# Rounding tiles to 256 bytes, staggering the compression between dense products, and taking one group of value products last

## The chip, the cores and the metric

The kernel runs on one core of a Trainium2 chip. It computes a hybrid attention layer and two further transformer layers for 512 tokens of width 1024, in float32. The metric is the device time of one execution in microseconds; the time before is the median of three runs.

## The reference, cut to what matters

```python
def hybrid_layer(x, mem, ...):
    x = x + 0.5 * swiglu_ffn(rmsnorm(x, ffn1_norm_g), ffn1_w_in, ffn1_w_out)     # d_ff = 2816
    h = rmsnorm(x, mix_norm_g)
    q, kv, nsa_g, conv_in, q_mem, merge_g = jnp.split(h @ w_in, split_points, axis=-1)
    kc, vc, ks, vs, kw, vw = ...                      # 4 groups of 64 columns each, 16 query heads
    k_cmp = rmsnorm(compress(kc, cmp_pe_k, cmp_w1_k, cmp_w2_k), k_norm_g)  # 31 blocks of 32 tokens, stride 16
    v_cmp = compress(vc, cmp_pe_v, cmp_w1_v, cmp_w2_v)      # silu(flat @ w1) @ w2
    o_nsa = nsa_attention(...)    # gated sum of compressed, selected and window attention
    o_conv = short_gated_conv(conv_in, conv_w, conv_b)
    o_mem = memory_attention(q_mem, mem, ...)               # 256 memory slots, 4 heads
    x = x + (g_nsa * o_nsa + g_conv * o_conv + g_mem * o_mem) @ w_out
    return x + 0.5 * swiglu_ffn(rmsnorm(x, ffn2_norm_g), ffn2_w_in, ffn2_w_out)

def second_block(x, p, ...):
    # layer 0: stick-breaking attention, layer 1: forgetting attention (softmax of q k + f_q - f_k);
    # both followed by swiglu and by h + sigmoid(rms_norm(h) @ w_gate) * (p @ w_proj)
```

## The kernel before

Everything lies transposed: 1024 features are eight tiles of 128 partitions, 512 tokens are the columns. A product in float32 precision is made of three matmuls: each operand is split into a rounded high part and the rest (`split`: ScalarE writes the high part, VectorE the difference), and `mm3` takes high by high, high by low and low by high. `dense` and `job` are the dense products: 128 rows of weights arrive by one DMA of 512 KB on SP's queue into a `raw` tile, are split into `wh` and `wl` (`weights`, three buffers each), and 24 matmuls of 512 columns follow, in which the stationary operand is a slice of `wh` or `wl` and the moving operand one of the sixteen tiles `h0h`, `h0l` ... `h7l` (the normalized activations). The second products of a feed-forward move the tiles `u0h` ... `u21l` (66 matmuls), `project` the tiles `m0h` ... `m7l`.

The stages follow one another: memory keys, feed-forward 1 (`ffn`), `memory`, `nsa`, `merge`, feed-forward 2, `stick`, feed-forward 3 with `ple`, `forget`, feed-forward 4 with `ple`. In `nsa` and `forget` dense products are cut into steps of three matmuls (`job`, `job_tok`) that `feed(n)` and `pace(upto)` put between the attention's instructions; `begin` starts their list, and each job's weights are asked for when the job before it starts. An attention loop runs over units (one head and one branch): `unit_scores`, softmax, `unit_scale` on GpSimd, and one unit later `unit_turn` (transposes and split of the probabilities) and `unit_out` (value products). In the loop the order of TensorE's instructions is that of the code (`pinned`); ahead of it the scheduler of the language may take what is ready first. `compress` is a generator: each `next(comp)` issues one more part of the compression of the keys and then the values. `nsa_cmp` does the same for the compressed scores of one group, in three parts.

A tile is given its place by its pool: tiles lie one behind another along the partition in the order of their first use, each as long as its width rounded up (`t`). `sb` is the first pool and holds `cols` (226 columns), `ones_d` (128), `eps` (one column) and then the sixteen `h` tiles; `wp`, with `raw`, `wh` and `wl`, follows behind `sb`. Pools on the right lie below a tile `edge` of 24 columns. In the program built of this kernel `h0h` begins at byte 2816 of the partition, `wh` at 69504, `u0h` of feed-forward 1 at 139136, `m0h` at 112512 in `merge`. The pools of `stick` and `forget` begin with the tile `rT` of four columns. In `memory` the tiles `mt` and `vm` lie an odd multiple of 256 bytes apart, by that program.

Of the kernel before, what the change touches and what calls it, by code (L numbers as in the profile page):

```python
# [28 lines left out]
LV = 1040  # L29
LU = 384  # L30


# [130 lines left out]
class Net:  # L163
    def __init__(self, ctx, tc, a, out):
        self.tc, self.nc, self.a, self.out = tc, tc.nc, a, out
        self.uid = self.turn = 0
        self.due, self.rest = [], []
        self.jobs, self.steps, self.pinned = None, 0, False
        self.tags = self.TAGS = ("d", "s", "t", "o")

        self.edge = ctx.enter_context(tc.tile_pool(name="edge", bufs=1, side="right"))
        self.edge.tile([P, 24], F32, name="edge", tag="edge")
        self.sb = ctx.enter_context(tc.tile_pool(name="sb", bufs=1))
        self.wp = ctx.enter_context(tc.tile_pool(name="wp", bufs=3))
        self.ps = ctx.enter_context(tc.tile_pool(name="ps", bufs=2, space=bass.MemoryType.PSUM))
        self.dr = ctx.enter_context(tc.tile_pool(name="dr", bufs=1, space=bass.MemoryType.DRAM))

    def t(self, pool, cols, tag, bufs=None, dt=F32, parts=P):
        self.uid += 1
        w = cols if pool is self.ps else -(-cols // 64) * 64 if dt == BF16 else -(-cols // 32) * 32  # L180
        x = pool.tile([parts, w], dt, name=f"{tag}_{self.uid}", tag=tag, bufs=bufs)
        return x if w == cols else x[:, :cols]
# [438 lines left out]

    def softmax_rows(self, pool, src, n, bias, stat, tag, bufs):

        nc = self.nc
        m = self.t(pool, 1, "sm", 8)
        p = self.t(pool, n, tag, bufs)
        if bias is None:
            nc.vector.tensor_reduce(m, src, axis=AX, op=ALU.min)
            nc.scalar.activation(p, src, AF.Exp, bias=m, scale=-1.0, accum_out=stat)
        else:  # L630
            nc.vector.tensor_tensor_reduce(  # L631
                out=p, in0=src, in1=bias, op0=ALU.add, op1=ALU.min, scale=1.0, scalar=3e38, accum_out=m)
            nc.scalar.activation(p, p, AF.Exp, bias=m, scale=-1.0, accum_out=stat)  # L633
        return p
# [47 lines left out]
    def memory(self):  # L682

        nc, tc = self.nc, self.tc
        with self.pool("mem", "left") as pool:
# [10 lines left out]
            for m in range(4):  # L696
# [15 lines left out]
                self.split(vm[0], vm[1], vr)  # L712
                st = self.t(pool, NT, "mst", 2)
                pr = []
                for i in range(NT):
                    sc = self.bank("s")[:, :NM]
                    q = slice(i * P, (i + 1) * P)
                    for c in range(2):
                        self.mm3(sc, qr[c][0][:, q], qr[c][1][:, q], kr[c][0], kr[c][1], c == 0, c == 1)
                    pr.append(self.softmax_rows(pool, sc, NM, None, st[:, i : i + 1], "mp", 8))  # L720
                nc.vector.reciprocal(st, st)
                pt = []
# [77 lines left out]
    def compress_flat(self, pool, tn, xs):  # L800
# [3 lines left out]
        ph = self.bank("o")[:, :256]  # L804
        for k in range(4):
            fl = self.t(pool, S, "cv", 4)
            fv = fl.rearrange("p (k g c) -> p k g c", g=4, c=32)
            nc.vector.memset(fl.rearrange("p (k c) -> p k c", c=32)[:, :, 31:], 0.0)
            for g in range(4):
                xa = xs[g // 2][64 * (g % 2) : 64 * (g % 2) + 64, :]  # L810
                for par in range(2):
                    h = slice(64 * par, 64 * par + 64)
                    xv = bass.AP(xa.tensor, xa.offset + par + 8 * k, [list(xa.ap[0]), [2, 4], [16, 31]])
                    nc.vector.tensor_tensor(  # L814
                        fv[h, :, g, :31], xv, pe[h, 4 * k : 4 * k + 4].unsqueeze(2).to_broadcast([64, 4, 31]), op=ALU.add)
# [62 lines left out]
    def unit_scores(self, pool, b, q, k, bias, mask=None):  # L878

        st = self.t(pool, NT, "st", 4)  # L880
        pr = []
        both = self.bank("s")
        for tiles in ((0, 1), (2,), (3,)):
# [9 lines left out]
            for i in tiles:  # L893
                n = (i + 1) * P
                pr.append(self.softmax_rows(pool, sc[i][:, :n], n, bias(n), st[:, i : i + 1], f"pr{i}", 2))
        return pr, st

# [17 lines left out]
    def unit_out(self, po, v, pt, first, last):  # L915

        ph, pl = pt
        for j in range(NT):
            n = S - j * P
            c = slice(self.PT0[j], self.PT0[j] + n)  # L920
            self.mm(po[:, j * P :], v(j), pl[:, c], start=first and j == 0, stop=False)
            self.mm(po[:, j * P :], v(j), ph[:, c], start=False, stop=last and j == NT - 1)

    def nsa(self):
        nc, tc = self.nc, self.tc
        self.hv = 1
        with self.pool("nsa", "right") as pool:
# [34 lines left out]
            def key(j):  # L962
                def post(ps):
                    k = self.t(pool, S, f"kx{j}") if j % 2 else self.t(pool, S, "cv", 4)
                    nc.vector.tensor_tensor(k, ps, self.rB, op=ALU.mult)
# [36 lines left out]
            self.feed(6)  # L1002
            for j in range(4):
                self.head_norm(ks[j], j, 1, st, self.col("kg"))
                self.feed(2)
            kn = [keys(0, br) for br in range(2)]
            self.feed(10)
            next(comp)
            st = self.head_stats(raw[0], self.sel64, 1, tag="o", fill=2)
            next(comp)  # L1010
            self.feed(6)
            for r in range(4):
                normed(0, r, st)
                if r == 2:
                    next(comp)
                self.feed(3)
            for _ in comp:
                self.feed(3)
# [12 lines left out]
            self.pace(8 * 12 + 8)  # L1031
            self.pinned = True
# [3 lines left out]
            for u in range(33):  # L1036
# [56 lines left out]

    def nsa_cmp(self, pool, a, b, qn, kc, G, pc):

# [3 lines left out]
        for z, y, w in ((kc[b], self.kcn[0], slice(0, P)), (kc[2 + b], self.kcn[1], h)):  # L1099
# [3 lines left out]
            nc.vector.tensor_copy(dst, y[w, 32 * g : 32 * g + 32].bitcast(F32).unsqueeze(1).to_broadcast([n, 4, 32]))  # L1103
        cb = self.t(pool, S, "cp", 1)
        for r in range(4):
# [9 lines left out]
        for i in range(NT):  # L1115
            self.tr(tp[:, i * P : (i + 1) * P], cb[:, i * P : (i + 1) * P])
        m = self.t(pool, 16, "cm", 2)
        rows = tp.rearrange("p (k c) -> p k c", c=32)
# [3 lines left out]
        nc.scalar.activation(cb, cb, AF.Exp, scale=-1.0)  # L1122
        z = self.t(pool, 16, "cz", 2)
        nc.vector.tensor_reduce(z, pv, axis=AX, op=ALU.add)
# [166 lines left out]
    def forget(self):  # L1291
# [3 lines left out]
        with self.pool("fox", "left") as pool:  # L1295
# [69 lines left out]
            self.feed(6)  # L1365
            base = self.steps
            rows = None
            fb = self.forget_bias(pool, 0)
            for u in range(17):
# [89 lines left out]
```

## Time and profile before

| | us |
|---|---|
| median of three runs | 2975.08 (2967.96 to 2980.09) |
| the profiled execution, its own time | 2973.13 |
| its span, first to last instruction | 2971.2 |
| TensorE (PE) busy in the span | 2898.9 |
| VectorE (DVE) busy | 1628.5 |
| ScalarE (ACT) busy | 1216.9 |
| GpSimd (POOL) busy | 247.9 |

The profiled execution lies 2 us below the median and the span 2 us below its own time. Lines of the profile name an engine, the source line (a helper's: L189 is every matmul, L194 every transpose, L208 and L218 the two halves of `split`), the operation, and output and inputs by tile name without buffer numbers. PEclk or "granted clock" is the share of TensorE's full 2.4 GHz. A matmul's own duration reaches past the start of the next; its pace is the distance from start to start.

### The profile page before, as it was taken

Reading aid. Unit: us, or ns where it says so; the run is one execution under the profiler, and the core shown is the slowest. Engines: PE = TensorE matmul, PEld = TensorE weight load, DVE = VectorE, ACT = ScalarE, POOL = GpSimd, SP = SyncE. Lnnn points to the kernel's source line nnn. Section 1 sums busy time; section 2 is a strip of 40 time slices with the busy share of each in tenths; the row PEclk is TensorE's granted clock in tenths of the full one; section 3 lists DMA queues with packets and bytes.
Section 4 is the critical chain, followed back from the end, with each engine's and each line's share of the span. In section 5 each row is a group of like instructions: output and inputs, shape, how many; then the busy total and the mean of one; then the engine's idle time right before and its main releaser. Section 6 shows DMA issues by size and latency. Waiting matters only on the chain.

```text
span 2971.2 us, 37172 instructions
## 1 busy us (share of the span) xinstructions
PE 2898.9 (98%) x13873; PEld 2369.6 (80%) x13874; DVE 1628.5 (55%) x2718; ACT 1216.9 (41%) x2078; POOL 247.9 (8%) x361
## 2 busy tenths in 40 slices
PE   8999999988999999999999999999999999999999
PEld 7888887766878888888888887888887777888887
DVE  7443345587677665344347877343357767544344
ACT  6322234344555544232235655222234556422223
POOL 0000000001224320000000000000003331000000
PEclk9999999999999999999999999999999999999999
DMA  7423342234333345222344345222334535522332
GB/s 239 107 92 96 104 130 89 96 105 124 94 105 93 91 151 172 97 93 91 112 122 117 86 123 185 97 92 91 97 110 127 141 93 157 180 92 93 94 93 98
DMA packets 133229, 339.19 MB, mean 114 GB/s; under 512 B 17415, under 2 KB 30215, under 8 KB 133048
## 3 DMA queue, kind: packets, MB, share of 16 engines
q1 hardware_dynamic: 132376, 335.49, 37.0%
q10 hardware_dynamic: 672, 1.32, 0.4%
q8 instruction: 109, 1.79, 0.2%
q14 instruction: 72, 0.59, 0.1%
HBM read 279.82 MB, written 28.61 MB: 104 GB/s over the span
## 4 chain that ended last, share of the span: by engine, by line
PE 72%; DVE 5%; issue 3%; ACT 1%; DMA 1%; POOL 0%; SPq 0%; DVEq 0%; POOLq 0%; ACTq 0%
PE d L189 27%; PE s L189 14%; PE o L189 14%; PE t L189 12%; PE t L194 2%; DVE wl L218 1%; DVE cv L814 1%; DMA qk<-xd 0%; DVE ptl L218 0%; DMA xd<-qk 0%; PE s L1278 0%; PE o L1288 0%; PE t L1278 0%; PE o L1289 0%; ACT wh L208 0%
## 5 line engine op out<-in xcount | busy, mean ns | idle before, releaser
L208 ACT ACTIVATE wh<-raw 128x1024 fp32r<-128x1024 f32 (+3 forms) x499 | 493.7, 990 | 1223.3 <-PE d L189 327.1
L218 DVE TENSOR_TENSOR wl<-raw,wh 128x1024 fp32r<-128x1024 f32 (+3 forms) x499 | 573.6, 1150 | 302.7 <-ACT wh L208 291.9
L900 POOL TENSOR_SCALAR pr<-pr,st 128x128 f32<-128x128 f32 x192 | 116.6, 627 | 245.0 <-DVE st L1374 97.8
L633 ACT ACTIVATE pr<-pr,sm 128x128 f32<-128x128 f32 x192 | 106.0, 553 | 64.1 <-DVE sm L631 63.6
L218 DVE TENSOR_TENSOR ptl<-t,pth 128x512 fp32r<-128x512 f32 x144 | 85.6, 596 | 32.6 <-ACT pth L208 30.7
L230 POOL TENSOR_TENSOR raw<-raw,cols 128x1024 f32<-128x1024 f32 x25 | 50.0, 2001 | 538.5 <-DMA xd<-x 472.1
L208 ACT ACTIVATE pth<-t 128x512 fp32r<-128x512 f32 x144 | 75.0, 522 | 48.5 <-PE t L194 47.8
L194 PE MATMUL t<-idn,pr 128*128 128x128 f32 x480 | 78.0, 278 | 3.0 <-DVE ptl L218 2.3
L194 PEld LDWEIGHTS t<-idn,pr 128*128 128x128 f32 x480 | 60.6, 143 | 21.6 <-DVE ptl L218 4.6
L631 DVE CUSTOM_DVE_ANT_0 pr<-s,tb 128x128 f32<-128x128 f32 (+3 forms) x128 | 57.9, 486 | 33.2 <-PE s L189 11.5
L189 PE MATMUL o<-ptl,V 128*128 128x512 f32 x192 | 60.3, 325 | 5.9 <-DVE ptl L218 5.7
L407 POOL MEMSET hrh<- 128x512 f32 (+2 forms) x10 | 4.7, 472 | 661.4 <-DVE wl L218 480.9
L189 PE MATMUL d<-h0h,wh 128*128 128x512 f32 x136 | 56.8, 418 | 0.0
L517 ACT ACTIVATE ta<-ta 128x512 f32<-128x512 f32 x88 | 55.5, 633 | 3.2 <-DVE ta L516 3.0
L189 PE MATMUL d<-h4h,wh 128*128 128x512 f32 x136 | 56.2, 413 | 0.0
L518 DVE TENSOR_TENSOR ta<-s,ta 128x512 f32<-128x512 f32 x22 | 15.2, 692 | 74.6 <-PE s L189 74.6
L189 PE MATMUL d<-h3h,wh 128*128 128x512 f32 x136 | 56.1, 412 | 0.0
L518 DVE TENSOR_TENSOR ta<-t,ta 128x512 f32<-128x512 f32 x22 | 15.2, 692 | 74.1 <-PE t L189 74.0
L189 PE MATMUL o<-pth,V 128*128 128x512 f32 x192 | 55.8, 324 | 0.0
L189 PE MATMUL d<-h2h,wh 128*128 128x512 f32 x136 | 55.5, 408 | 0.0
L482 ACT ACTIVATE on<-o 64x512 f32<-64x512 f32 x48 | 28.6, 595 | 65.8 <-PE o L189 51.1
L189 PE MATMUL d<-h1h,wh 128*128 128x512 f32 x136 | 55.4, 407 | 0.0
(2163 smaller groups left out, 8719.8 us busy)
## 6 DMA issues: line engine op xcount, KB each, us to landing
raw<-in_f_in_dram SPq DMA_DIRECT2D x176, 512.0 KB
raw<-in_f_out_dram SPq DMA_DIRECT2D x64, 512.0 KB
raw<-in_f_out_dram SPq DMA_DIRECT2D x32, 384.0 KB
raw<-in_w_mg_dram SPq DMA_DIRECT2D x24, 512.0 KB
raw<-in_w_cv_dram SPq DMA_DIRECT2D x24, 512.0 KB
xd<-x SPq DMA_DIRECT2D x32, 256.0 KB
x<-xd SPq DMA_DIRECT2D x32, 256.0 KB
raw<-in_w_pg_dram SPq DMA_DIRECT2D x16, 512.0 KB
```

The lines of the kernel that those rows point to most:

```text
L189: i = self.nc.tensor.matmul(out, lhs, rhs, **kw)
L194: i = self.nc.tensor.transpose(out, src, self.ident)
L208: nc.scalar.activation(h, src, AF.Copy, scale=1.0 if scale is None else scale)
L218: eng.tensor_tensor(lo, src, hb, op=ALU.subtract)
L230: nc.gpsimd.tensor_tensor(v, v, gain.unsqueeze(2).to_broadcast([P, gain.shape[1], n]), op=ALU.mult)
L482: self.nc.scalar.activation(dst[h], po[64:], AF.Copy)
L517: nc.scalar.activation(ta, ta, AF.Silu)
L518: nc.vector.tensor_tensor(ta, pb, ta, op=ALU.mult)
L631: nc.vector.tensor_tensor_reduce(out=p, in0=src, in1=bias, op0=ALU.add, op1=ALU.min, scale=1.0, scalar=3e38, accum_out=m)
L633: nc.scalar.activation(p, p, AF.Exp, bias=m, scale=-1.0, accum_out=stat)
L814: nc.vector.tensor_tensor(fv[h, :, g, :31], xv, pe[h, 4 * k : 4 * k + 4].unsqueeze(2).to_broadcast([64, 4, 31]), op=ALU.add)
L900: self.nc.gpsimd.tensor_scalar(pr[i], pr[i], st[:, i : i + 1], 1.0, op0=ALU.mult, op1=ALU.mult)
```

## The change

Tiles in SBUF are rounded up to 64 columns of 4 bytes instead of 32 (`t`). The softmax minima move from tiles of their own (`sm`) into the tile of the sums (`st`, `mst`), and `cz` into `cm`. `compress_flat` prepares the rows and asks for the weights of part k + 1 when part k's matmuls are issued, and yields once before the first and once behind the last; odd parts use the tiles `q4s0` and `q4s1`. `nsa` calls `next(comp)` between feeds of 8 steps (one whole dense product), the values' products come after the first convolution, `nsa_cmp` is interleaved for both groups (a second tile for the second), and 126 steps instead of 104 are done when the unit loop starts. `unit_turn` no longer feeds one step between the first and the second group of transposes; `unit_out` takes the groups in the order 0, 1, 3, 2; more steps are held back behind `unit_out` (2 in `nsa`, 4 in `forget`, before 1), and `forget` feeds 2 steps more after the statistics and 2 more after the second norm. The number of matmuls, transposes, splits and DMAs is the same.

```diff
 def t(self, pool, cols, tag, bufs=None, dt=F32, parts=P):
-    w = cols if pool is self.ps else -(-cols // 64) * 64 if dt == BF16 else -(-cols // 32) * 32
+    w = cols if pool is self.ps else -(-cols // 128) * 128 if dt == BF16 else -(-cols // 64) * 64
...
 def softmax_rows(self, pool, src, n, bias, st, i, tag, bufs):
-    m = self.t(pool, 1, "sm", 8)
+    m, stat = st[:, NT + i : NT + i + 1], st[:, i : i + 1]
...
 def compress_flat(self, pool, tn, xs):
     ph = self.bank("o")[:, :256]
-    for k in range(4):
+    def rows(k):
         fl = self.t(pool, S, "cv", 4)
...
-        fh, flo = self.pair(pool, "pt", S, 1)
+        if k % 2:
+            fh, flo = (self.t(pool, S, f"q4s{z}", dt=F32R) for z in range(2))
+        else:
+            fh, flo = (z[:, :S] for z in self.pair(pool, "pt", 1280, 1))
         self.split(fh, flo, fl)
-        wh, wl = self.weights(self.a["w_c1"]["kv".index(tn), k])
+        return fh, flo, self.weights(self.a["w_c1"]["kv".index(tn), k])
+    nxt = rows(0)
+    yield
+    for k in range(4):
+        fh, flo, (wh, wl) = nxt
         for c in range(4):
...
-        if k < 3:
-            yield
+        nxt = rows(k + 1) if k < 3 else None
+        yield
...
 def unit_turn(self, pool, pr):
-        self.feed((0, c0 // 512)[c0 > 0])
+        self.feed(2 * (tiles == (2,)))
...
 def unit_out(self, po, v, pt, first, last):
-    for j in range(NT):
+    for j in (0, 1, 3, 2):
...
 def nsa(self):
-    jobs = [key(j) for j in range(4)] + [query(0, r) for r in range(4)] + [values(0), self.job(self.a["w_g"][0], self.h, gates), values(1)]
-    jobs += self.conv(0, pool) + self.conv(1, pool)
+    jobs = [key(j) for j in range(4)] + [query(0, r) for r in range(4)] + [self.job(self.a["w_g"][0], self.h, gates)]
+    jobs += self.conv(0, pool) + [values(0), values(1)] + self.conv(1, pool)
...
+    next(comp)
     for k in range(4):
         self.feed(8)
         next(comp)
+    self.feed(8)
+    next(comp)
     st = self.head_stats(ks, self.sel64, 1, fill=2)
-    self.feed(6)
+    next(comp)
+    self.feed(8)
+    next(comp)
...
-    cmps = [self.nsa_cmp(pool, 0, b, [qn[0, r] for r in range(4)], kc, G, pc) for b in range(2)]
-    next(cmps[0])
-    self.feed(6)
+    cmps = [self.nsa_cmp(pool, 0, b, [qn[0, r] for r in range(4)], kc, G, pc, ("cp", "on")[b]) for b in range(2)]
+    for n in (6, 10):
+        for b in range(2):
+            next(cmps[b])
+        self.feed(n)
     for b in range(2):
-        next(cmps[b])
-        self.feed(6)
-        for _ in cmps[b]:
-            pass
-        if b == 0:
-            next(cmps[1])
-        self.feed(6)
-    self.pace(8 * 12 + 8)
+        next(cmps[b], None)
+    self.pace(126)
...
-            self.pace(upto - 1)
+            self.pace(upto - 2)
             self.nsa_out(pool, V, pc, pt, *rows[1:])
...
 def forget(self):
     st = self.head_stats(xs[0], self.sel64, 1, pool=pool, tag="o", fill=3)
-    self.feed(7)
+    self.feed(9)
     kq = {0: norm(0, st)}
     self.feed(4)
     kq[1] = norm(1, st)
-    self.feed(6)
+    self.feed(8)
...
-                self.pace(upto - 1)
+                self.pace(upto - 4)
                 self.forget_out(pool, m + later, V, pt, *rows[1:])
```

## Rows read from the trace of the kernel before

**Rows 1.** The page's first part: busy time of each engine in the whole span

```profile
PE 2898.9 (98%) x13873; PEld 2369.6 (80%) x13874; DVE 1628.5 (55%) x2718; ACT 1216.9 (41%) x2078; POOL 247.9 (8%) x361
```

**Rows 2.** Windows: first products of the four feed-forwards, nsa's opening, nsa's loop, forget

```profile
core 0: us, PE busy (x) PEld busy (x) DVE busy (x) ACT busy (x) POOL busy (x), PEclk, DMA share, GB/s
77.00:307.00 230.00, 230.00 (x992) 186.45 (x991) 94.77 (x108) 68.31 (x85) 0.00 (x0) 1.00 0.32 97
1173.00:1414.00 241.00, 241.00 (x1034) 193.90 (x1033) 97.18 (x110) 73.77 (x92) 0.00 (x0) 1.00 0.29 94
1841.00:2070.00 229.00, 229.00 (x987) 185.70 (x986) 93.40 (x107) 69.10 (x85) 0.00 (x0) 1.00 0.31 99
2545.00:2791.00 246.00, 246.00 (x1054) 197.61 (x1053) 99.62 (x114) 73.67 (x92) 0.00 (x0) 1.00 0.32 105
590.00:762.00 172.00, 145.40 (x776) 118.80 (x774) 123.19 (x260) 76.34 (x124) 14.86 (x19) 0.96 0.38 110
762.00:1078.00 316.00, 308.53 (x1613) 255.97 (x1612) 220.53 (x513) 175.14 (x407) 101.53 (x142) 0.99 0.33 94
2242.00:2545.00 303.00, 285.39 (x1563) 231.38 (x1562) 226.76 (x414) 170.56 (x345) 92.01 (x99) 0.98 0.47 138
```

**Rows 3.** The chain that ended last, in order of time: start us, us, what

```profile
566.43 22.39 PE d L189 x96
...
1134.06 5.44 PE d L189 x24
...
1178.73 5.60 PE d L189 x24
...
1428.91 14.96 PE o L189 x66
...
1847.18 5.57 PE t L189 x24
```

**Rows 4.** TensorE's timeline in merge's `project`: start us, us, instruction

```profile
1129.36 0.39 PE L189 MATMUL o<-m1l,wh 128*128 128x512 f32 x1
...
1131.85 0.39 PE L189 MATMUL o<-m5h,wh 128*128 128x512 f32 x1
```

**Rows 5.** The same view in the last `project` of forget

```profile
2531.95 0.39 PE L189 MATMUL o<-m4h,wh 128*128 128x512 f32 x1
...
2534.74 0.40 PE L189 MATMUL d<-m4h,wh 128*128 128x512 f32 x1
```

**Rows 6.** The same view in memory, value products of one head

```profile
518.70 0.39 PE L189 MATMUL o<-mt1l,vmh 128*128 128x512 f32 x1
...
520.06 0.39 PE L189 MATMUL o<-mt1h,vml 128*128 128x512 f32 x1
```

**Rows 7.** TensorE's waits in 590:760 (us in total, times, longest us)

```profile
PE t L194 <- POOL cp L1128: 7.5, 2, 4.7
PE o L189 <- ACT pth L208: 3.1, 4, 1.2
PE o L189 <- ACT wh L208: 3.0, 2, 1.8
PE t L194 <- DVE cp L1112: 2.9, 1, 2.9
...
PE o L189 <- DVE wl L218: 1.4, 1, 1.4
```

**Rows 8.** Groups of instructions by line, 588:760: the additions that build the compression's rows

```profile
L814 DVE TENSOR_TENSOR cv<-q2s,cols 64x124 f32<-64x124 f32 x32 | 11.6, 361 | 0.7
```

**Rows 9.** Tile `cp` in 588:762: duration ns min/median/max, first and last start us

```profile
L1112 DVE TENSOR_TENSOR cp<-s,cp x2: 691/692/692, 709.2 to 739.3; 128x512 f32<-128x512 f32 x2
...
L1128 POOL TENSOR_TENSOR cp<-cp,cz x2: 1044/1046/1049, 719.5 to 744.3; 128x512 f32<-128x512 f32 x2
```

**Rows 10.** Windows around two stretches with a lower granted clock (columns of rows 2)

```profile
738.00:750.00 12.00, 5.21 (x21) 4.48 (x22) 4.92 (x10) 2.96 (x6) 3.11 (x5) 0.62 0.43 122
844.00:852.00 8.00, 6.54 (x21) 4.59 (x22) 6.96 (x15) 2.36 (x5) 4.22 (x4) 0.68 0.24 76
```

**Rows 11.** TensorE's waits in the whole span (columns of rows 7)

```profile
PE o L189 <- DVE ptl L218: 5.7, 9, 1.2
PE s L189 <- DVE x L422: 5.2, 9, 2.1
...
PE t L194 <- DVE ptl L218: 2.3, 3, 1.4
```

More of the change, by code (lines that the diff above doesn't have):

```diff
@@ L30 @@
 LU = 384
+EDGE = 24
 def _stat(w):
@@ L171, in __init__ @@
         self.edge = ctx.enter_context(tc.tile_pool(name="edge", bufs=1, side="right"))
-        self.edge.tile([P, 24], F32, name="edge", tag="edge")
+        self.edge.tile([P, EDGE], F32, name="edge", tag="edge")
         self.sb = ctx.enter_context(tc.tile_pool(name="sb", bufs=1))
@@ L619, in transpose_rows, with softmax_rows @@
             nc.vector.tensor_copy(dst[:, i : i + 1], ps[:, :1])
-    def softmax_rows(self, pool, src, n, bias, stat, tag, bufs):
+    def softmax_rows(self, pool, src, n, bias, st, i, tag, bufs):
         nc = self.nc
-        m = self.t(pool, 1, "sm", 8)
+        m, stat = st[:, NT + i : NT + i + 1], st[:, i : i + 1]
         p = self.t(pool, n, tag, bufs)
@@ L712, in memory @@
                 self.split(vm[0], vm[1], vr)
-                st = self.t(pool, NT, "mst", 2)
+                st = self.t(pool, 2 * NT, "mst", 2)
                 pr = []
@@ L719, in memory @@
                         self.mm3(sc, qr[c][0][:, q], qr[c][1][:, q], kr[c][0], kr[c][1], c == 0, c == 1)
-                    pr.append(self.softmax_rows(pool, sc, NM, None, st[:, i : i + 1], "mp", 8))
-                nc.vector.reciprocal(st, st)
+                    pr.append(self.softmax_rows(pool, sc, NM, None, st, i, "mp", 8))
+                nc.vector.reciprocal(st[:, :NT], st[:, :NT])
                 pt = []
@@ L878, in unit_scores @@
     def unit_scores(self, pool, b, q, k, bias, mask=None):
-        st = self.t(pool, NT, "st", 4)
+        st = self.t(pool, 2 * NT, "st", 4)
         pr = []
@@ L894, in unit_scores @@
                 n = (i + 1) * P
-                pr.append(self.softmax_rows(pool, sc[i][:, :n], n, bias(n), st[:, i : i + 1], f"pr{i}", 2))
-        return pr, st
+                pr.append(self.softmax_rows(pool, sc[i][:, :n], n, bias(n), st, i, f"pr{i}", 2))
+        return pr, st[:, :NT]
     def unit_scale(self, pr, st):
@@ L921, in unit_out @@
             self.mm(po[:, j * P :], v(j), pl[:, c], start=first and j == 0, stop=False)
-            self.mm(po[:, j * P :], v(j), ph[:, c], start=False, stop=last and j == NT - 1)
+            self.mm(po[:, j * P :], v(j), ph[:, c], start=False, stop=last and j == 2)
     def nsa(self):
@@ L963, in post @@
                 def post(ps):
-                    k = self.t(pool, S, f"kx{j}") if j % 2 else self.t(pool, S, "cv", 4)
+                    k = self.t(pool, S, f"kx{j}") if j % 2 else self.t(pool, S, "pr3", 2)
                     nc.vector.tensor_tensor(k, ps, self.rB, op=ALU.mult)
@@ L1005, in nsa @@
                 self.feed(2)
+            next(comp)
             kn = [keys(0, br) for br in range(2)]
-            self.feed(10)
-            next(comp)
             st = self.head_stats(raw[0], self.sel64, 1, tag="o", fill=2)
             next(comp)
-            self.feed(6)
+            self.feed(8)
+            next(comp)
             for r in range(4):
                 normed(0, r, st)
[L1014 to L1018, printed above, removed]
-            pc = {}
-            cmps = [self.nsa_cmp(pool, 0, b, [qn[0, r] for r in range(4)], kc, G, pc) for b in range(2)]
-            next(cmps[0])
-            self.feed(6)
-            for b in range(2):
-                next(cmps[b])
-                self.feed(6)
-                for _ in cmps[b]:
-                    pass
-                if b == 0:
-                    next(cmps[1])
-                self.feed(6)
-            self.pace(8 * 12 + 8)
+                self.feed(2)
+            next(comp, None)
+            self.feed(8)
+            pc = {}
+            cmps = [self.nsa_cmp(pool, 0, b, [qn[0, r] for r in range(4)], kc, G, pc, ("cp", "on")[b]) for b in range(2)]
[3 more added lines that the diff above has]
+                self.feed(n)
+            for b in range(2):
+                next(cmps[b], None)
+            self.pace(126)
             self.pinned = True
@@ L1092, in nsa_out, with nsa_cmp @@
             self.nc.sync.dma_start(self.od[64 * hd : 64 * hd + 64, :], o[h])
-    def nsa_cmp(self, pool, a, b, qn, kc, G, pc):
+    def nsa_cmp(self, pool, a, b, qn, kc, G, pc, tag="cp"):
         nc = self.nc
@@ L1103, in nsa_cmp @@
             nc.vector.tensor_copy(dst, y[w, 32 * g : 32 * g + 32].bitcast(F32).unsqueeze(1).to_broadcast([n, 4, 32]))
-        cb = self.t(pool, S, "cp", 1)
+        cb = self.t(pool, S, tag, 1)
         for r in range(4):
@@ L1116, in nsa_cmp @@
             self.tr(tp[:, i * P : (i + 1) * P], cb[:, i * P : (i + 1) * P])
-        m = self.t(pool, 16, "cm", 2)
+        mz = self.t(pool, 32, "cm", 2)
+        m, z = mz[:, :16], mz[:, 16:]
         rows = tp.rearrange("p (k c) -> p k c", c=32)
@@ L1122, in nsa_cmp @@
         nc.scalar.activation(cb, cb, AF.Exp, scale=-1.0)
-        z = self.t(pool, 16, "cz", 2)
         nc.vector.tensor_reduce(z, pv, axis=AX, op=ALU.add)
@@ L1364, in forget @@
             kq[1] = norm(1, st)
-            self.feed(6)
+            self.feed(8)
             base = self.steps
```

## The prediction

> **What bounds the kernel now.** I read the busy times first: TensorE is busy in 2898.9 of 2971.2 us, no other engine in more than 55% [rows 1]. So a gain has two sources: the 72 us in which TensorE is idle, and the pace at which it works through its matmuls. I read the windows stage by stage next. In the feed-forwards it is busy without a gap, but the same 128x512 matmul has different paces: 230 us / 992 = 231.9 ns in the first, 233.1, 232.0 and 233.4 ns in the others [rows 2]. Then the chain of waits, because it counts whole products: 24 matmuls on the `h` tiles take 5.57 to 5.60 us (232 to 233 ns each), 24 on merge's `m` tiles 5.44 us and 66 on the `u` tiles 14.96 us, which is 226.7 ns both times [rows 3]. Shape, type, clock and weights are alike; the moving tile's place is not. Last, the idle time: nsa's opening has 172 - 145.4 = 26.6 us of it, nsa's loop 7.5, forget 17.6 [rows 2]; that is 52 of the 72 us.
>
> **Part 1, rounding to 256 bytes.** It removes and adds no instruction; it moves tiles. In the built kernel `h0h` is at byte 2816 and `wh` at 69504: 66688 apart, 260.5 x 256, so they differ by 128 modulo 256, because `eps`, one column, takes 128 bytes. All `h`, `wh` and `wl` tiles are multiples of 256 long, so this holds for every `h` product. `u0h` (139136) and merge's `m0h` (112512) are whole multiples of 256 from `wh`, and these are the fast products. The best test is inside one function: `project` runs at (1131.85 - 1129.36) / 11 = 226.4 ns in merge [rows 4] and at (2534.74 - 2531.95) / 12 = 232.5 ns in forget [rows 5], where `rT`, rounded to 128 bytes, shifts the `m` tiles by 128. I conclude that the pace depends on the distance between moving and stationary tile modulo 256.
>
> After the change `eps` takes 256 bytes, `h` begins 1792 = 7 x 256 behind the start of `sb`, and `sb` has 56320 = 220 x 256 bytes before `wp` begins (219 x 256 before). Pools on the right still end at `edge`, so `u` stays where it fits; `rT` becomes 256. Every dense pair is then a multiple of 256 apart. Now 256, though, where `u` and merge's `m` were 0 modulo 512. The memory stage has pairs an odd multiple of 256 apart: there six gaps take (520.06 - 518.70) / 6 = 226.7 ns once the run goes [rows 6]. So 256 is enough.
>
> The sum. Feed-forwards, 44 products of 24 = 1056 matmuls each: (231.9 + 233.1 + 232.0 + 233.4 - 4 x 226.7) x 1056 = 25 us. Merge's gates, both `ple` gates and the memory stage, 8 + 16 + 16 products = 960 matmuls at about 233 ns (96 of them in 22.39 us [rows 3]): 6 us; I take 5.5, as memory's are interrupted. Mixed stages: nsa has 49 products on `h`, stick 16 and forget 17, and 8 `project` products each: 98 x 24 = 2352 matmuls, 13.9 us if all reach the fast pace. But memory's run begins with slow gaps, and feeds of two to four steps (6 to 12 matmuls) between attention matmuls are mostly beginning: lower end 0, upper 13.9; I take 5, nearer the lower, since interruption is the rule there. Part 1: 35.5 us, bounds 25 to 45 if the reading is right. No other engine stops it: the `u` products already go on at the fast pace with the same splits and DMAs.
>
> One rule speaks against this. The Trainium skill, SBUF — State Buffer, "SBUF: two separate sides", says that TensorE and ScalarE never wait on anyone at SBUF, and under "A bandwidth-pool intuition that's wrong" that weight loads have a read port of their own. By that, placement is free and part 1 is worth 0; the two paces of one function [rows 4, 5] disagree with it.
>
> **Part 2, nsa's opening.** Compression's matmuls now find rows, split and weights ready. One part needs eight additions at 0.36 us (64 for both tensors, half of them in [rows 8]) and a split, some 4.5 us of VectorE and ScalarE, ahead of twelve matmuls. TensorE waited for them 3.1 + 3.0 + 1.4 = 7.5 us [rows 7]. A whole dense product, 5.5 us, now covers them: I take 6.5. The weights' DMA, also moved ahead on SP's queue, is counted with them: it takes the third of three `raw`/`wh`/`wl` buffers while two hold the running and the next product, so it just fits; what it costs if it doesn't is the same wait as now. The additions stand ahead of a dense evacuation on VectorE, which is 72% busy in that window (123.2 of 172); the evacuation's bank is one of two, which gives a product's time.
>
> Compressed scores: TensorE waits 7.5 us for GpSimd's product and 2.9 for the sum [rows 7]; for the second group the chain from the sum to GpSimd's end runs 739.3 to 745.4, 6.1 us, nearly uncovered [rows 9]. Both groups side by side and ten steps (30 matmuls, 7 us) behind cover it; two chains share VectorE, so I take 8 of 10.4. These stalls also pull the clock: in 738:750 the granted share is 0.62, which means 9 us at the 1.2 GHz level behind the longest stall [rows 10]; over the opening 0.96 of 172 us, 14 us at half, of which about 9 were work: 4.5 us lost, I take 3.5. Norms, `hid` and the gates' transposes still wait as now. Less 2 us for new waits: 16 us. Bounds: 0 (the scheduler places them no better) and 26.6 + 4.5 = 31.
>
> **Part 3, the loops.** Taking group 2 last covers its split with six value products. Its price now: 5.7 us of waits in both loops [rows 11]. The step taken out between the first two groups shortens the time to the third, which needs the first group's bank: 2.3 us of waits now, in 3 of 48 units [rows 11]. 22 steps fewer are left for nsa's 32 units (282 instead of 304, 0.5 us per unit). More steps behind `unit_out` cover the next scores, which wait 5.2 us for the norms [rows 11]. Bounds +8 and -6; I take 0, since gains and losses are of one size. Minima in the tile of the sums are other columns: the same instructions on the same engines, so 0; if the two engines took turns over that tile it would lengthen softmax, and rival D says where it shows.
>
> **The sum.** 35.5 + 16 + 0 = 51.5 us off 2973.1 = 2921.6; the median lies 2 us above the profiled execution, so about **2923 us**.
>
> **Rivals.** A: placement is nothing, and `h` is slow for another reason, such as what stands beside it. Against it: `project` twice. The time: 2975 - 16 = 2959. By the Trainium skill's rule above this is the outcome; the traces leave it little.
> B: the opening gains nothing: scheduler and VectorE's 72% move the stall to the norms and to `hid`. For it: much of the 26.6 us is many small waits, four of which I name. 2975 - 35.5 = 2939.
> C: the period is 512 after all. Then `u` (2112 matmuls) and merge's `m` (192) fall to the slow pace, 2304 x 5.9 = +13.6 us, and `h` stays slow: 2975 + 13.6 - 16 = 2973. Against it: [rows 6].
> D, the slower end: the units lose their cover. Place: third group of transposes or the next scores, in each of 48 units. Price: the longest such wait is 1.4 to 2.1 us [rows 11]; behind such a stall the clock is half, as at 844:852, where the share is 0.68 [rows 10]. It decides from 51.5 / 48 = 1.1 us per unit; at 1.4 the time is 2975 - 51.5 + 67 = 2990. Against it: the units have 8.8 steps each, 6 us.
>
> **How the numbers follow.** The forecast 55% (its own range 2905 to 2937), B 23%, A 14%, C 5%, D 3%. Three runs of this kernel spread by 0.4%, so less than 0.5% (15 us) can't be told from no change; the line is 2960. A lies on it, so half of it counts as no change: faster 0.55 + 0.23 + 0.07 = 0.85, same 0.07 + 0.05 = 0.12, slower 0.03. The range runs from 2903 (part 1 at 45, part 2 at 25, part 3 at 2) to 2959 (A).
>
> **What would show it.** Right: 24 matmuls on `h` take 5.44 us on the chain in all four feed-forwards, each of which ends 5 to 7 us sooner; 66 on `u` stay at 14.96; nsa's opening has under 15 us of idle time, with no wait for GpSimd above 2 us and no stretch at 1.2 GHz as long as 10 us. Wrong: `h` products still at 5.57 to 5.60 (A); 66 on `u` at 15.3 (C); the waits of [rows 7] back under other names (B); a wait in every unit, or ScalarE and VectorE taking turns in softmax (D).

## The result, and the profile after

The changed kernel takes 2932.35 us (median of four runs, 2930.51 to 2934.46); the kernel before took 2977.01 in the runs made with it. The ratio is 0.9855, 95% interval 0.9832 to 0.9879: 44.7 us less, where 51.5 were forecast (2923 us, range 2903 to 2959). The profiled execution took 2931.1 us with a span of 2929.3, so the spans differ by 41.9 us.

The busy times come first, as in [rows 1]; the line numbers are higher by one here (L190 is every matmul, L195 every transpose, L219 the second half of `split`).

```profile
PE 2858.3 (98%) x13873; PEld 2367.6 (81%) x13874; DVE 1615.2 (55%) x2718; ACT 1212.9 (41%) x2078; POOL 238.7 (8%) x361
```

TensorE is busy for 40.6 us less with as many matmuls. It is idle for 2929.3 - 2858.3 = 71.0 us, against 72.3 before: the idle time has not become less, it has moved. The windows show where (the first products of two feed-forwards, nsa's opening, nsa's loop, forget up to its last value product, and twelve microseconds of the opening; columns of [rows 2], whose stretch of forget has its last `project` too, without idle time):

```profile
75.00:300.00 225.00, 225.00 (x994) 186.34 (x993) 93.87 (x107) 69.86 (x87) 0.00 (x0) 1.00 0.33 100
2520.00:2745.00 225.00, 225.00 (x995) 186.36 (x994) 91.97 (x105) 67.22 (x84) 0.00 (x0) 1.00 0.31 100
582.00:724.00 142.00, 132.13 (x729) 110.78 (x730) 104.81 (x208) 67.84 (x106) 11.83 (x15) 0.98 0.45 132
724.00:1069.00 345.00, 319.26 (x1663) 264.42 (x1661) 220.64 (x534) 181.19 (x423) 98.53 (x146) 0.99 0.31 89
2216.00:2484.00 268.00, 254.99 (x1453) 209.56 (x1452) 201.24 (x381) 154.17 (x323) 90.45 (x100) 0.99 0.45 131
...
584.00:596.00 12.00, 8.24 (x28) 6.75 (x29) 8.08 (x24) 0.73 (x1) 0.00 (x0) 0.72 0.30 100
```

The feed-forwards go at 225 / 994 = 226.4 ns per matmul, all at one pace now; [rows 2] had 231.9 to 233.4. nsa's opening has 9.9 us of idle time instead of 26.6, forget 13.0 instead of 17.6, and nsa's loop 25.7 instead of 7.5. The chain of waits (start us, us, what) counts the products, beside [rows 3]:

```profile
1168.24 5.44 PE d L190 x24
...
1411.68 14.96 PE o L190 x66
...
1830.25 5.44 PE t L190 x24
...
2526.86 5.44 PE t L190 x24
```

24 matmuls on `h` take 5.44 us in feed-forwards 2, 3 and 4 and 66 on `u` still take 14.96. The last `project` of forget, which was the slow one of the two [rows 5], on TensorE's timeline:

```profile
2487.72 0.39 PE L190 MATMUL o<-m4h,wh 128*128 128x512 f32 x1
...
2490.44 0.39 PE L190 MATMUL d<-m4h,wh 128*128 128x512 f32 x1
```

Twelve gaps in 2.72 us are 226.7 ns; there it had been 232.5. TensorE's waits in the opening (582:724) answer [rows 7]:

```profile
PE t L619 <- DVE rT L620: 4.1, 1, 4.1
PE d L190 <- DVE wl L219: 1.7, 2, 0.9
...
PE t L195 <- POOL on L1138: 0.3, 1, 0.3
PE t L195 <- POOL cp L1138: 0.2, 1, 0.2
```

The 7.5 us for GpSimd, the 7.5 for the compression's rows and weights and the 2.9 for the sum are gone. One wait is new: four small transposes of `rB` (L619), whose copies stand on VectorE behind the compression's additions, which now come sooner; the granted clock in 584:596, which holds most of that wait and what follows it, is 0.72. Over the whole span the waits are, beside [rows 11]:

```profile
PE t L195 <- DVE ptl L219: 21.7, 23, 3.5
PE s L190 <- ACT wh L209: 5.8, 2, 5.4
...
PE o L190 <- DVE ptl L219: 2.0, 4, 0.6
```

The first row was 2.3 us in three waits. It is the transposes' wait for a bank that an earlier group's split still reads; 17.7 of the 21.7 us lie in nsa's loop, in 18 waits. One of them on the timeline of all engines:

```profile
798.51 1.04 PE L195 MATMUL t<-idn,pr 128*128 128x128 f32 x8
...
799.43 1.22 DVE L219 TENSOR_TENSOR wl<-raw,wh 128x1024 fp32r<-128x1024 f32 x1
...
800.53 0.39 PE L190 MATMUL d<-h2h,wl 128*128 128x512 f32 x1
...
800.57 0.69 DVE L219 TENSOR_TENSOR ptl<-t,pth 128x512 fp32r<-128x512 f32 x1
...
801.31 0.44 PE L195 MATMUL t<-idn,pr 128*128 128x128 f32 x2 [0.39 <-DVE ptl L219]
```

The eight transposes at 798.51 are those of the first two groups. The split of the first group begins on VectorE at 800.57 only, behind the split of a dense weight (1.22 us), and ends at 801.26. The third group's two transposes start at 801.31. The two steps ahead of them, six matmuls, end too soon to cover that.

From the starts of named matmuls in each trace I have the lengths of three stages, for all kernels that follow. The opening runs from memory's last value product to the first of nsa's loop, the loops from their first value product (nsa) or scores (forget) to their last value product; us:

| kernel | nsa's opening | nsa's loop | forget's loop |
|---|---|---|---|
| before | 187.7 | 323.5 | 211.7 |
| after | 170.3 | 339.4 | 201.6 |
| rounding alone | 189.2 | 320.8 | 212.5 |
| after, feed as before | 168.1 | 323.6 | 195.3 |
| rounding and opening alone | 169.3 | 324.9 | 210.9 |
| feed as before, one step held back | 169.2 | 325.0 | 205.7 |
| feed 0, 2, 2 | 168.1 | 325.0 | 211.1 |
| feed as before, `rT` late | 163.7 | 326.5 | 195.8 |
| order of products and 104 steps as before | 166.8 | 331.7 | 195.5 |

So of the 41.9 us, the opening gave 17.4 and forget's loop 10.1, and nsa's loop took 16.0. The loops don't hold the same work before and after. A step is three matmuls, some 0.68 us. Between the first transposes and the last value product of nsa's loop stand 256 steps instead of 262; the six others run ahead of it. Between the first scores and the last value product of forget stand 153 instead of 160, which is 4.8 us of its gain: four of the seven run ahead of it, where forget's start is only 0.5 us longer than with rounding alone, and three behind it, where its last `project` takes 1.4 us longer although its matmuls are faster. The rest is 25.4 us in the four feed-forwards (5.9, 7.0, 5.5 and 7.0 us, from the last matmul of the product before to the last one on `u`), and 6.4 in memory, merge, `stick`, the gates and forget's start.

### The profile page after: what moved, and what is told of

Read it like the earlier page. It is cut to its first block, busy times and chain, and to the rows that moved or that the text cites. A ratio compares the mean times of both kernels' runs of the same rounds, so it can differ in the third digit from the quotient of the medians.

```text
span 2929.3 us, 37143 instructions
## 1 busy us (share of the span) xinstructions
PE 2858.3 (98%) x13873; PEld 2367.6 (81%) x13874; DVE 1615.2 (55%) x2718; ACT 1212.9 (41%) x2078; POOL 238.7 (8%) x361
## 4 chain that ended last, share of the span: by engine, by line
PE 63%; DVE 4%; issue 2%; DMA 1%; ACT 1%; POOL 0%; SPq 0%; DVEq 0%; ACTq 0%; POOLq 0%
PE d L190 22%; PE s L190 13%; PE o L190 13%; PE t L190 11%; PE t L195 1%; DMA qk<-xd 1%; DVE wl L219 1%; DVE pr L632 1%; DVE ptl L219 1%; DMA xd<-qk 1%; PE s L1288 0%; PE t L1288 0%; PE o L1298 0%; POOL mo L1172 0%; PE o L1299 0%
## 5 line engine op out<-in xcount | busy, mean ns | idle before, releaser
L219 DVE TENSOR_TENSOR wl<-raw,wh 128x1024 fp32r<-128x1024 f32 (+3 forms) x499 | 576.7, 1156 | 302.7 <-ACT wh L209 299.8
L634 ACT ACTIVATE pr<-pr,st 128x128 f32<-128x128 f32 x192 | 106.1, 553 | 68.8 <-DVE st L632 67.9
L910 POOL TENSOR_SCALAR pr<-pr,st 128x128 f32<-128x128 f32 x192 | 106.2, 572 | 244.5 <-DVE st L1384 72.2
L195 PE MATMUL t<-idn,pr 128*128 128x128 f32 x480 | 70.5, 277 | 24.5 <-DVE ptl L219 21.7
L219 DVE TENSOR_TENSOR ptl<-t,pth 128x512 fp32r<-128x512 f32 x144 | 83.3, 595 | 19.4 <-ACT pth L209 18.5
L195 PEld LDWEIGHTS t<-idn,pr 128*128 128x128 f32 x480 | 54.9, 141 | 43.0 <-DVE ptl L219 33.6
L632 DVE CUSTOM_DVE_ANT_0 pr<-s,tb 128x128 f32<-128x128 f32 (+3 forms) x128 | 57.8, 486 | 33.9 <-PE s L190 15.8
L190 PE MATMUL o<-ptl,V 128*128 128x512 f32 x192 | 61.5, 331 | 3.3 <-DVE ptl L219 2.0
L484 DVE TENSOR_TENSOR on<-o,on 64x512 f32<-64x512 f32 x48 | 32.7, 681 | 46.7 <-ACT on L483 46.5
L190 PE MATMUL o<-pth,V 128*128 128x512 f32 x192 | 56.7, 321 | 0.0
L190 PE MATMUL d<-h3h,wh 128*128 128x512 f32 x136 | 55.8, 411 | 0.0
L190 PE MATMUL d<-h2h,wh 128*128 128x512 f32 x136 | 55.8, 410 | 0.0
L190 PE MATMUL d<-h0h,wh 128*128 128x512 f32 x136 | 55.1, 405 | 0.4 <-DVE q2s L794 0.4
L190 PE MATMUL d<-h4h,wh 128*128 128x512 f32 x136 | 55.3, 407 | 0.0
L190 PE MATMUL d<-h0h,wl 128*128 128x512 f32 x136 | 53.5, 393 | 1.7 <-DVE wl L219 1.7
```

Of the source, the lines that this page charges most:

```text
L190: i = self.nc.tensor.matmul(out, lhs, rhs, **kw)
L195: i = self.nc.tensor.transpose(out, src, self.ident)
L219: eng.tensor_tensor(lo, src, hb, op=ALU.subtract)
L484: self.nc.vector.tensor_tensor(dst[h], po[:64], dst[h], op=ALU.add)
L632: nc.vector.tensor_tensor_reduce(out=p, in0=src, in1=bias, op0=ALU.add, op1=ALU.min, scale=1.0, scalar=3e38, accum_out=m)
L910: self.nc.gpsimd.tensor_scalar(pr[i], pr[i], st[:, i : i + 1], 1.0, op0=ALU.mult, op1=ALU.mult)
```

## The experiments

All ratios are to the kernel before, with 95% intervals. Its medians were 2972.8 us beside experiments 1, 2, 5 and 6, 2969.4 beside 3, 4, 7 and 8, and 2971.0 beside 9 to 12.

**1. Rounding alone.** The kernel before with the rounding and, so that the pools fit, the minima in the tile of the sums and `cz` in `cm`, as in the change; nothing is staggered.

```diff
-        w = cols if pool is self.ps else -(-cols // 64) * 64 if dt == BF16 else -(-cols // 32) * 32
+        w = cols if pool is self.ps else -(-cols // 128) * 128 if dt == BF16 else -(-cols // 64) * 64
```

> The kernel before with the rounding to 256 bytes alone (the minima and cz share tiles, which makes room for it). Theory P (the pace of a 128x512 matmul hangs on the distance of its two tiles modulo 256 bytes): 24 matmuls on h take 5.44 us on the chain in all four feed-forwards, 66 on u stay at 14.96, and the time is 33 to 40 us under the kernel before (about 2940). Rival A (placement is nothing): h products stay at 5.57 to 5.60 and the time stays within 5 us of the kernel before.

Measured: 2937.5 us, 0.9887 (0.9868 to 0.9905). The `h` products in its chain:

```profile
1208.09 5.44 PE o L189 x24
```

The feed-forwards give 4.6, 7.0, 3.9 and 7.0 us, the opening and the loops nothing beyond 3 us. The rounding is worth 35.3 us by the medians and 31.1 by the spans.

**2. `h` displaced by 128 bytes in the changed kernel.** A gap of 128 bytes ahead of the `h` tiles and one behind them; everything else of the change stays.

```diff
+        sb.tile([P, 32], F32, name="gap0", tag="gap0")
         self.h = [self.pair(sb, f"h{c}") for c in range(KC)]
+        sb.tile([P, 32], F32, name="gap1", tag="gap1")
```

> The changed kernel with a gap of 128 bytes ahead of the sixteen h tiles and one of 128 bytes behind them; everything else stays where it fits. P: only the h products slow down, to 5.57 to 5.60 us for 24, u stays at 14.96, and forget's last project (m tiles) stays at the fast pace; the time is 30 to 36 us over the changed kernel (about 2965). A: no difference, 2932.

Measured: 2965.2 us, 0.9979 (0.9969 to 0.9989), 33 us more than the changed kernel. The chain:

```profile
1412.32 14.97 PE t L190 x66
...
2570.88 5.60 PE s L190 x24
```

The products on `h` are slow again, those on `u` are not, though `u` now lies a multiple of 512 from the weights and lay 256 beside one before. The `m` products stay at 227 ns, and the opening keeps its gain (170.0 us against 187.7). So the place of one operand makes the pace, and an odd multiple of 256 is as good as an even one.

**3 and 4. `h` displaced by 64 and by 32 bytes.** The same with gaps of 16 and 48, or of 8 and 56 columns, each timed once.

> The changed kernel with the h tiles displaced by 64 bytes against the weights (a gap tile of 64 bytes before them, one of 192 behind them); everything else stands where it stood. Displaced by 128 bytes the feed-forwards' first products went at 232 to 233 ns per matmul and the kernel took 2965 us; displaced by 0 at 226.7 ns and 2932. Theory E (only a whole multiple of 256 is fast): 24 matmuls on h take 5.57 us or more, the kernel 2960 to 2970 us or above. Rival G (the cost grows with the distance): about half of it, 24 matmuls in 5.50 us, 2945 to 2952 us. Rival N (only an odd multiple of 128 collides): 5.44 us and 2932.

> The same with 32 bytes instead of 64. Theory E: 5.57 us or more for 24 matmuls on h, 2960 to 2970 us or above. Rival G: a quarter of the cost of 128 bytes, 5.47 us, 2938 to 2943 us. Rival N: 5.44 us and 2932.

Measured: 2937.0 us with 64 bytes, 2969.4 with 32. The chains, first of 64 and then of 32 bytes:

```profile
2546.30 5.49 PE s L190 x24
```

```profile
2590.59 5.60 PE d L190 x24
```

None of the three theories holds. At 64 bytes a matmul takes 228.8 ns, a third of the way from 226.7 to 233.3; at 32 it costs as much as at 128. Neither "only a whole 256" nor "the more the farther" describes that, and I have no rule for it.

One rival is left by the products on `h`, `u` and `m`: the moving tile's own place could make the pace, not how it lies to the weights, since the weights were never shifted by other than multiples of 256. The products for the values answer it, for there the weights move, 256 columns at a time, and slices of `h` are stationary. The first and the last of the same 96 matmuls in `stick`, in the changed kernel and with `h` displaced by 64 bytes:

```profile
1634.57 0.28 PE L190 MATMUL d<-wh,h0h 128*128 128x256 f32 x1
...
1645.96 0.28 PE L190 MATMUL d<-wh,h7l 128*128 128x256 f32 x1
```

```profile
1639.71 0.28 PE L190 MATMUL d<-wh,h0h 128*128 128x256 f32 x1
...
1650.50 0.28 PE L190 MATMUL d<-wh,h7l 128*128 128x256 f32 x1
```

95 gaps take 11.39 and 10.79 us, 119.9 and 113.6 ns each. The moving tiles lie as before modulo 256, only the stationary ones are displaced, and the pace changes: it does not hang on the moving tile alone. And here the whole multiple of 256 is not the best place; 64 bytes beside it is 5% faster (with 128 and 32 bytes the same run has 118.6 and 118.3 ns). What "good" is depends on the form of the matmul.

**5. The feed restored.** In the changed kernel 0, 1 and 2 steps stand again ahead of the three groups of transposes.

```diff
-            self.feed(2 * (tiles == (2,)))
+            self.feed((0, c0 // 512)[c0 > 0])
```

> The changed kernel with the step between the first two groups of transposes put back (feeds 0, 1, 2 as before). Theory T (the third group of transposes waits for the bank that the first group's split has not yet freed): TensorE's waits for ptl ahead of transposes fall from 21.7 us to under 6, and the time falls by 12 to 20 us to about 2916. Rival H (the loop loses its cover because more steps are held back behind unit_out): the waits move to other instructions and the time moves by less than 5 us.

Measured: 2912.2 us, 0.9801 (0.9783 to 0.9819), 20 us less than the changed kernel. nsa's loop goes from 339.4 to 323.6 us, forget's from 201.6 to 195.3. The wait did not fall under 6 us, but from 21.7 to:

```profile
PE t L195 <- DVE ptl L219: 8.1, 9, 2.8
```

**6. The order of the value products restored** (0, 1, 2, 3 instead of 0, 1, 3, 2).

```diff
-        for j in (0, 1, 3, 2):
+        for j in range(NT):
```

> The changed kernel with the value products in the order 0, 1, 2, 3 again. If taking group 2 last hides its split: waits of the value products for ptl rise from 2.0 us to 6 to 12, time 3 to 8 us over the changed kernel. Rival: the split is there in time in either order, since the held-back and fed steps cover it, and the time moves by less than 3 us.

Measured: 2934.0 us, 0.9875 (0.9860 to 0.9889), 1.6 us over the changed kernel, which is within the intervals. The order is worth under 3 us; its wait is

```profile
PE o L190 <- DVE ptl L219: 3.6, 8, 0.7
```

instead of 2.0 us in four.

**7. Rounding and opening alone,** both loops as before.

```diff
-            self.pace(upto - 2)
+            self.pace(upto - 1)
...
-                self.pace(upto - 4)
+                self.pace(upto - 1)
...
-            self.feed(9)
+            self.feed(7)
...
-            self.feed(8)
+            self.feed(6)
```

(and the feed and the order of the two experiments above).

> The kernel before with the rounding and the new opening of nsa, and both loops as before (feeds of 0, 1 and 2 steps in a turn, groups 0, 1, 2, 3, one step held back, forget's feeds of 7 and 6). Theory S (the opening's gain of 21 us stands by itself; the loops were neither helped nor hurt by it): 2937.5 - 21 = 2914 to 2918 us, nsa's loop within 3 us of the rounded kernel, forget's units as before. Rival L (the loop pays for the 126 steps done ahead of it: its units run short of steps): nsa's loop 5 to 10 us longer than in the rounded kernel, 2921 to 2927 us.

Measured: 2922.0 us, 0.9837 (0.9822 to 0.9852). Against rounding alone the opening is 19.9 us shorter, although it does six steps more; the loop is 4.0 us longer, although six steps of 0.68 us are no longer in it. Its waits in 722:1052:

```profile
PE t L195 <- DVE ptl L219: 8.7, 9, 2.8
```

The kernel with rounding alone has 2.3 us of them there, with the same code in the loop. The opening's gain stands by itself (S), but the loop does pay some 8 us for it; the time lies in L's range. Why is open: fewer steps, or other products beside the same units (the list's order was changed too); experiment 12 puts both back.

**8. One step held back** in both loops of the kernel of experiment 5, instead of two and four.

```diff
-                    self.pace(upto - 2)
+                    self.pace(upto - 1)
...
-                    self.pace(upto - 4)
+                    self.pace(upto - 1)
```

> The kernel with the feed restored (2912 us) with one step held back behind the value products in both loops, instead of two in nsa and four in forget. In that kernel forget's loop was 16.4 us shorter than in the kernel before, nsa's loop as long as before. Theory H (forget's gain is the hold-back: steps behind the value products cover the next scores' wait): forget's loop loses 8 to 15 us, the kernel takes 2920 to 2927 us. Rival F (it is the four steps more that forget issues ahead of its loop, and the order of the groups): within 4 us of 2912. If in nsa holding back two steps rather than one costs something, nsa's loop is shorter here by 2 to 4 us.

Measured: 2922.1 us, 0.9840 (0.9823 to 0.9856). Forget's loop loses 10.4 us, as H expected, nsa's loop 1.4 (no gain from holding back less). Some 2 of the 10.4 us come back behind the loop: it holds three steps more, which ran behind its last value product before. So the hold-back is worth some 8 us in forget. TensorE's waits in 2250:2490:

```profile
PE s L190 <- DVE st L632: 4.9, 6, 1.5
PE s L190 <- DVE x L423: 3.6, 9, 0.7
```

With four steps held back the same two waits, in that window of experiment 5, are

```profile
PE s L190 <- DVE x L423: 2.1, 5, 0.6
...
PE s L190 <- DVE st L632: 1.4, 4, 0.6
```

The steps behind the value products cover the next scores' waits for the norms and for softmax; these two rows are 5.0 of the 8 us, the rest is not assigned.

**9. Feed 0, 2, 2** in the kernel of experiment 5.

```diff
-            self.feed((0, c0 // 512)[c0 > 0])
+            self.feed(2 * (c0 > 0))
```

> The kernel with the feed restored (0, 1 and 2 steps ahead of the three groups of transposes; 2912 us), with two steps ahead of the second group instead of one: 0, 2, 2. Between the first and the third group stand then four steps instead of three (two in the changed kernel). The third group's wait for the first group's split was 21.7 us with two steps and 8.1 with three. Theory B (that wait is set by the steps between the two groups): under 3 us with four, the kernel 2905 to 2909 us. Rival Q (the step is taken from behind the second split and from behind the value products, where it is then missing): the waits of the value products and of the next scores grow by as much, 2910 to 2916 us.

Measured: 2920.8 us, 0.9834 (0.9821 to 0.9848), 9 us more than with three steps. Its waits:

```profile
PE s L190 <- DVE st L632: 8.8, 6, 3.7
...
PE o L190 <- DVE ptl L219: 6.1, 7, 1.6
...
PE t L195 <- DVE ptl L219: 2.8, 2, 2.1
```

The bank's wait fell as B said, to 2.8 us, but the step is missing behind the products: the two other rows were 4.3 and 2.0 us, and forget's loop is 15.8 us longer, with six steps more in it (4.1 us) that ran behind it before. Q is right, and by more than it said.

**10. `rT` late** in the kernel of experiment 5, and **11. both edits.**

```diff
             rT = self.t(pool, NT, "rT")
-            self.transpose_rows(rT, self.rB)
...
+            self.transpose_rows(rT, self.rB)
             pc = {}
```

> The kernel with the feed restored, with the four small transposes of rB (tile rT) issued ahead of the compressed scores instead of ahead of the compression. In the changed kernel and in this one TensorE waits 4.1 us for their copies, which stand on VectorE behind the additions of the compression's rows. Theory V (the wait is made by the place in the queue): it goes, the start of the opening is 3 to 4 us sooner, 2907 to 2910 us. Rival W (VectorE is behind by then in any case, and TensorE waits at the compression's first matmuls or the next product instead): 2911 to 2914 us.

> The last two edits together. Theories B and V: 2901 to 2906 us. Q and W: 2910 to 2916 us; one of each: 2906 to 2910 us.

Measured: 2905.7 us, 0.9785 (0.9771 to 0.9798) with `rT` late; 2917.3, 0.9819 (0.9805 to 0.9832) with both. The wait of 4.1 us does not occur in either, and the opening is 4.4 us shorter (163.7 against 168.1); nsa's loop is 2.9 us longer, and the spans, 2907.0 us here and 2906.0 in experiment 5, are alike. By the medians it is the fastest kernel here, but its interval overlaps that of experiment 5. V is right for the wait; what it is worth in the end these runs don't settle. With both edits the time lies above every range that was given: V and Q together were to take 2906 to 2910 us, and the fourth step costs 11.6 us over `rT` late alone.

**12. Products in the order of before and 104 steps** in the kernel of experiment 5. In this kernel the statistics of the second half's query heads are issued before the fourth head's product is done and leave that head out (two matmuls fewer).

```diff
-            jobs = [key(j) for j in range(4)] + [query(0, r) for r in range(4)] + [self.job(self.a["w_g"][0], self.h, gates)]
-            jobs += self.conv(0, pool) + [values(0), values(1)] + self.conv(1, pool)
+            jobs = [key(j) for j in range(4)] + [query(0, r) for r in range(4)] + [values(0), self.job(self.a["w_g"][0], self.h, gates), values(1)]
+            jobs += self.conv(0, pool) + self.conv(1, pool)
...
-            self.pace(126)
+            self.pace(104)
```

> The kernel with the feed restored, with the list of dense products in the order of the kernel before (values 0, gates, values 1, then the convolutions) and 104 steps done ahead of nsa's loop instead of 126, so that up to 22 more steps, 15 us of matmuls, are left for its units. Theory L (the loop runs short of steps between its transposes because they were done ahead): opening and loop together 4 to 8 us shorter, 2904 to 2908 us. Rival K (the steps only change places): opening and loop together within 2 us, 2910 to 2914 us.

Measured: 2915.5 us, 0.9816 (0.9803 to 0.9830). 270 steps instead of 256 lie between the loop's first transposes and its last value product, so 14 moved, not 22. Opening and loop together take 498.5 us instead of 491.7: neither L (shorter) nor K (equal). In the opening (600:724) an old wait is back:

```profile
PE t L195 <- POOL cp L1138: 4.7, 1, 4.7
```

The steps done ahead of the loop were the cover of the compressed scores. The loop is 8.1 us longer than in experiment 5 with 9.5 us of steps more in it, so little over 1 us of its idle time went. The transposes' wait for `ptl` is still 6.0 us in this loop (6.9 in experiment 5, 2.3 with rounding alone): the list's order, which is as before here, and the number of steps, which is higher than before, don't explain by themselves what experiment 7 left open.

## Why the prediction was right, and where not

**Part 1 (35.5 us, 25 to 45): right.** Shown from both sides: alone it is worth 35.3 us by the medians, and undone for `h` alone it costs 33. The feed-forwards, forecast at 25 us, give 25.4 in the changed kernel. Of the 5 us taken for the mixed stages 3.4 came with rounding alone (forget with its start and `project` 1.7, nsa 1.1, `stick` 0.6). A (2959) is refuted by experiments 1 and 2, C (2973) by `u`, which stays at 14.96 us at an odd multiple of 256. The rule as the prediction has it holds for the matmuls of 512 columns; with 256 columns another place is better (experiments 3 and 4). The Trainium skill, SBUF — State Buffer, "SBUF: two separate sides", says that TensorE never waits on anyone at SBUF. The prediction took from it that placement is free; the 33 us of experiment 2 show that it isn't. The minima in the tile of the sums cost nothing, as was said: the softmax's exponentials take 553 ns on ScalarE in both pages.

**Part 2 (16 us, 0 to 31): right in mechanism, the term was too small.** The opening is 17.4 us shorter in the profile, with six steps (4.1 us) more in it: 21.5. Every wait of [rows 7] that was named is gone, GpSimd's are 0.5 us together and idle time is 9.9 us, under the 15 that the test named. The lowest clock is 0.72 in twelve microseconds, 6.7 us at the lower level, under the ten. The 2 us for new waits came as one wait of 4.1, for `rT`. Rival B, by which the opening gains nothing, fell with that.

**Part 3 (0, from +8 to -6): the step that failed.** "I take 0, since gains and losses are of one size" put two loops together that went opposite ways. nsa's loop lost 16.0 us, or 20 if the six steps moved out of it are counted; forget's gained 10.1, of which 2.0 are the three steps that now run behind it. Together -8 us, or -12 so counted: beyond the lower bound. The reason was in the text, but sized wrongly: "the step taken out between the first two groups shortens the time to the third" was priced at the 2.3 us that the wait cost before. Experiment 5 gives the price: 20 us. A wait that three steps just covered was read as if its present remainder were its size. Rival D named the place. Its mechanism came true in 18 waits of nsa's loop, but at 17.7 us over 32 units, half a microsecond each, below the 1.1 from which it would have decided.

The gains that were set against it: the order of the groups, priced at up to 5.7 us, is worth under 3 (experiment 6); the steps held back are worth some 8 us in forget and 1.4 in nsa (experiment 8). They also cover a wait that no term of part 3 had: that of the scores for the softmax's minima (L631 before, L632 after), 4.2 us in forget before and 1.2 after.

**"22 steps fewer" was wrong.** 104 was only a lower limit, and the feeds ahead of it had already passed it. Between the loop's first transposes and its last value product stand 262 steps before and 256 after, six fewer.

**The sum.** 51.5 us were forecast, 41.9 came by the spans and 44.7 by the medians: about 3 us less than forecast from the rounding, 5 more from the opening as counted above, and 12 lost in the loops. That the time lies so near the forecast is luck in part: the errors of parts 2 and 3 have opposite signs.

**What stays open:** why nsa's loop waits 8.7 us instead of 2.3 for the bank behind the new opening when its own code is unchanged (experiment 7; experiment 12 speaks against the two reasons given there), the course of the pace between 0 and 128 bytes, and whether the distance alone counts: no run moved both tiles of a dense product together.

## What to carry to other kernels

Compare the same instruction's pace in several stages before looking at waits: a pace that differs by 3% at one shape and clock was worth more here than all waits removed, and a tile of one column had caused it. When cover is taken from one place to give to another, price the wait as it would be without the cover, not as what is left of it with the cover in place; here 2.3 us became 21.7. Test edits to a schedule one by one: of those in the two loops one lost 20 us, one gained some 8, and the kernel without the first is faster than the one before and the changed one (2912.2 us; 2905.7 with the small transposes moved as well). Count the steps on both sides of a stage's marks before calling a shorter stage a gain: 4.8 of forget's 10.1 us were steps that now run outside of it.

## What the runs showed of the hardware

The pace of 128x512 float32 matmuls, each with its own weight load, depends on how the moving tile lies to the stationary one: 226.7 ns at a whole multiple of 256 bytes, even or odd, 228.8 ns at 64 bytes beside it, 233.3 ns at 32 and at 128. With 256 columns the order is another: 119.9 ns at a whole multiple, 113.6 at 64 bytes beside it. The pace does not change at once with the place. In the kernel before, feed-forward 1's first matmuls on `u`, well placed, follow badly placed ones on `h`: their first ten gaps take 2.31 us (314.84 to 317.15), the next ten 2.27. The six matmuls of a `ple` product on its tiles `pt`, a whole multiple of 256 from the weights in both kernels, have 232 ns per gap between badly placed `h` products (experiment 2) and 227 between well placed ones (the changed kernel).

The granted clock in 584:596 of the changed kernel, which holds a wait of 4.1 us but for its first 0.4, was 0.72. In the eleven later stretches of twelve microseconds in the opening, with waits of at most 1.1 us, it was 1.00, and so it was in 618:630 of the kernel before, with waits of 2.1, 1.4 and 0.3 us.
